# Moving one projection of the cross attention's V from the head of a mixing stage into its gate loop

## The chip, the cores and the metric

The kernel runs on one core of a Trainium2 chip (trn2). The metric is the device time of one execution in microseconds (us). Three executions of the kernel before gave 2055.84, 2061.27 and 2065.23 us, the median is 2061.27 us. The profile is of one further execution, which took 2056.62 us.

## The reference

Two transformer blocks run one after the other on 256 tokens of width 1024, in float32. The second one has two layers, and each layer is this:

```python
x = x + 0.5 * rms_norm(swiglu(rms_norm(x), ffn1_w13[l], ffn1_w2[l]))
h = rms_norm(x, mix_norms[l, 0])
y = token_mixing(h, ...)          # retention, latent attention, differential attention
x = x + rms_norm(y, mix_norms[l, 1])
h = rms_norm(x, cross_norms[l, 0])
m = rms_norm(mem, cross_norms[l, 2])          # 256 memory tokens, not dependent on x
x = x + rms_norm(cross_attention(h, m, cross_wq[l], cross_wkv[l], cross_wo[l]))
x = x + 0.5 * rms_norm(swiglu(rms_norm(x), ffn2_w13[l], ffn2_w2[l]))
```

At the end of token_mixing three branches are gated, added and projected:

```python
proj = einsum('bsnw,nwd->bsnd', branches, w_branch)   # three branches, 512 -> 1024 each
gates = sigmoid(gate_logits)                          # 3 x 1024 columns of h @ w_in
return sum(gates * proj, axis=n) @ w_out
```

In cross_attention `kv = m @ w_kv` has 2048 columns: K of four heads of 256 columns, then V of four heads. It needs the memory alone, so it can be computed long before h is known.

## The kernel before, in words

**Products.** Each float32 operand is split into a high part (`wh`, a cast to fp32r on ACT, L209) and a low part (`wl`, the rest, by DVE, L210). A product is three matmuls: high*high, and the two mixed ones (`mm3`, L242 to L244). In `proj_fm` the weights are the stationary operand and 256 tokens are streamed; in `proj_tm` the tokens are stationary (two halves of 128, t = 0 and t = 1) and up to 512 weight columns are streamed.

**Weights.** `weights` (L213) loads 512 KB into one of three buffers `raw` with a DMA that SP issues, and splits it into one of three buffers `wh` and `wl`. The three are shared by everything outside the inner part of the feed-forward stages. `self.parts` says in how many pieces a tile is split (PK = 4 gives two pieces of 128x512 for a tile of two 512-column rows, PM = 1 gives one of 128x1024).

**K and V ahead of time.** `kv_job` (L1013) holds a list of chunks of `kv`. Chunks 0 to 3 are K of a head each; chunk 4 is V of heads 0 and 1: 512 columns for both halves of tokens, 8 steps of the contraction, 48 matmuls of 128x512 in all, into two banks of PSUM with the tag "p", then two copies on ACT (L1021) to `raw40` and `raw41`. `fill(n)` computes the next n chunks. `run` calls fill(2) in the feed-forward stage before (chunks 0, 1), fill(2) at the head of the layer's first feed-forward (2, 3) and fill(6) at the head of `mix2`, which is chunk 4, since no other is left. Chunk 5 is computed within `cross`.

**mix2.** `norm_T` normalizes and transposes the tokens: squares on ACT and DVE (L335), the root on POOL (L343), the scaling on DVE (L351), 16 transposes on PE (L368), and the split of their result into `xth` and `xtl`. Then comes the fill, then `mla_low` (a `proj_tm` of 416 columns), the projections and the three attentions. At the end stand the gates: for branch 2, four times `gate` and four times `branch`; then, for branches 1 and 0 and each jj of four, `gate` (48 matmuls of 128x256, weights in two tiles, a tanh on ACT) and `branch` (24 matmuls, one tile, two operations on DVE). `ret_att`, which branch 0 needs, is given high priority. `merge` and the product with `w_out` follow.

**What sets the order.** The engines run in order. The order on each engine is set when the kernel is built, by a scheduler that takes instructions by their place in the program where their operands are ready by its own estimate of time; `high_priority` moves a place ahead. Buffers of a tag go round in the program's order.

Of the kernel before, what the change touches and what calls it, by code (L numbers as in the profile page):

```python
# [16 lines left out]
D = 1024  # L17
KD = 8
# [4 lines left out]
P1, PC, PF, PM, PK = 1, 2, 2, 1, 4  # L23
NEARLY = 4
STAG = 120
TAIL = 3
FTAIL = 3
TAILS = (3, 6)
# [82 lines left out]
class Core:  # L111
# [134 lines left out]
    def mm(self, out, a, b, start=True, stop=True):  # L246
        self.nc.tensor.matmul(out, a, b, start=start, stop=stop, skip_group_check=True)  # L247
# [56 lines left out]

    def down_all(self, xt, src, ntail=TAIL):
        with self.pool("tail", ntail) as pool:
            acc, step = self.down_steps(src, len(xt), pool, ntail)
            for k in range(len(xt)):
                step(k, xt[k])
        return acc  # L310
# [180 lines left out]

    def cross(self, xs, gx, w_q, w_o, mt, w_kv, raw, mid=None, ntail=TAIL):

# [477 lines left out]
    def mix1(self, gate_pool, load, early, side):  # L971
# [5 lines left out]
        with self.pool("m1") as pool, self.wides():  # L977
# [19 lines left out]
            for hf in range(2):  # L997
                with self.tc.high_priority(offset=self.tc.cur_priority - start - hf * STAG):
                    self.rwkv(lup[hf], krv[hf], hf, zp[:, 2 * hf:2 * hf + 2, :])
# [13 lines left out]
    def kv_job(self, mt, w_kv, raw):  # L1013

        todo = list(raw)

        def fill(n):
            for _ in range(min(n, len(todo))):
                i = todo.pop(0)
                for r, b in zip(raw[i], self.kv_chunk(mt, w_kv, i)):  # L1020
                    self.nc.scalar.copy(out=r.rearrange("p i c -> p (i c)"), in_=b)  # L1021

        return fill

    def run(self, out):
        a, nc = self.a, self.nc
        n2 = a["cross_norms_2"]
        side = ExitStack()
        mem = {}

        def open_side():
            self.rawp = side.enter_context(self.pool("raw", side="right"))
            self.pad(self.rawp, 224)
            mem["R"] = self.mkR(side.enter_context(self.pool("mt", side="right")))

        def early(pool):
            mem["mt"] = self.norm_T(self.load_x(a["mem"][0]), a["norm_mem_g"][0])
            mem["raw"] = {i: [pool.tile([128, 2, T], F32, name="raw_b1%d" % i)] for i in range(NEARLY)}
            self.kv_job(mem["mt"], a["w_ckv"][0], mem["raw"])(8)

        def prepare(l):

            mt = self.mem_T(a["mem_2"][0], n2[l, 2], mem["R"])
            rt = lambda n: self.rawp.tile([128, 2, T], F32, tag=n, name=n)
            raw = {i: [rt("raw%d%d" % (i, j)) for j in range(1 if i < 4 else 2)] for i in range(5)}
            mem.update(mt=mt, raw=raw, fill=self.kv_job(mt, a["cross_wkv_2"][l], raw))

        fill = lambda n: mem["fill"](n)

        def start_ffn():  # L1050
            fill(2)
            self.rope_tables()

        with self.pool("b1") as pool:
            with self.pool("gt") as gp:
                xs = self.mix1(gp, lambda names: self.load_const(names, pool), lambda: early(pool), open_side)
            with self.pool("cr") as cp:
                self.phase(cp)
                acc = self.cross(xs, a["norm_x_g"][0], a["w_cq"][0], a["w_co"][0], mem["mt"], a["w_ckv"][0],
                                 mem["raw"], mid=lambda: prepare(0))  # L1060
            xs = self.residual(xs, acc)
            acc = self.ffn(xs, a["norm_ffn_g"][0], a["w_ffn_in"][0], a["w_ffn_out"][0], self.conv_hidden,
                           start_ffn)
        xs = self.final_norm(self.residual(xs, acc), a["norm_final_g"])
        with self.pool("b2") as pool:
            self.load_const(["ret"], pool)
            for l in range(2):
                acc = self.ffn(xs, a["ffn1_norms_2"][l, 0], a["ffn1_w13_2"][l], a["ffn1_w2_2"][l], self.swiglu_hidden,
                               lambda: fill(2))
                xs = self.residual(xs, acc, a["ffn1_norms_2"][l, 1], 0.5)  # L1070
                acc = self.mix2(l, xs, lambda: fill(6))
                xs = self.residual(xs, acc, a["mix_norms_2"][l, 1])
                with self.pool("cr") as cp:
                    self.phase(cp)
                    acc = self.cross(xs, n2[l, 0], a["cross_wq_2"][l], a["cross_wo_2"][l], mem["mt"],
                                     a["cross_wkv_2"][l], mem["raw"], mid=(lambda: prepare(1)) if l == 0 else side.close, ntail=TAILS[l])
                xs = self.residual(xs, acc, n2[l, 1])
                acc = self.ffn(xs, a["ffn2_norms_2"][l, 0], a["ffn2_w13_2"][l], a["ffn2_w2_2"][l], self.swiglu_hidden,
                               (lambda: fill(2)) if l == 0 else None)
                xs = self.residual(xs, acc, a["ffn2_norms_2"][l, 1], 0.5)  # L1080
        for t in range(2):
            for h in range(2):
                s = slice(h * 512, (h + 1) * 512)
                nc.sync.dma_start(out=out[t * 128:(t + 1) * 128, s], in_=xs[t][:, s])
# [274 lines left out]
        V.tensor_tensor(out=o, in0=o, in1=sg.rearrange("p t (h c) -> p (t h) c", h=4), op=ALU.mult)  # L1359
        self.to_branch(bp, o, 1)  # L1360

    def mix2(self, l, xs, fill):
        nc, a = self.nc, self.a
        xt = self.norm_T(xs, a["mix_norms_2"][l, 0])
        self.parts = PK
        fill()
        self.parts = PM
        w_in = a["w_in_2"][l]
        with self.pool("m2") as pool, self.wides():
            self.pad(pool, 448)  # L1370
            R = self.phase(pool)
            bps = [Pair(R("bh", [128, 4, T], F32R, 2), R("bl", [128, 4, T], F32R, 2)) for n in range(3)]
            low = self.mla_low(l, xt)
            nlam = self.diff_lam(l)
            dft = R("dft", [128, 8, T])
            for q in range(2):
                bs = self.proj_tm(self.wcols(w_in, 1952 + q * 512, 512), xt, 512)
                self.rotated(bs, dft[:, q * 4:q * 4 + 4, :], 8, 8, 48, 0)
            heads = self.mla_half(l, low, 0)
            self.mla_att(heads, bps[1][:, 0:2, :])  # L1380
            dv = self.tokens(w_in, 2976, xt)
            self.diff_att(l, dft, dv, nlam, bps[2])
            rft = self.s4([128, 4, T], F32, "rft")
            self.rotated(self.proj_tm(self.wcols(w_in, 0, 512), xt, 512), rft, 8, 32, 0, 1)
            heads = self.mla_half(l, low, 1)
            self.mla_att(heads, bps[1][:, 2:4, :])
            rv = self.tokens(w_in, 512, xt)
            sg = self.ret_gate(l, xt)
            order = (2, 1, 0)
            gates = {}  # L1390

            def gate(n, jj):
                b = self.proj_fm(self.wcols(w_in, 3488 + n * D + jj * 256, 256), xt)
                g = R("gm" if n == order[0] else "gate", [128, 2, T], bufs=4 if n == order[0] else 2)
                nc.scalar.activation(out=g.rearrange("p i c -> p (i c)"), in_=b, func=AF.Tanh, scale=0.5)
                gates[n, jj] = g

            def branch(n, jj):
                y = [bps[n][:, k, :] for k in range(4)]
                b = self.proj_fm(self.wcols(a["w_branch_2"][l, n], jj * 256, 256, 4), y)  # L1400
                g, m = gates[n, jj], gates[order[0], jj]
                nc.vector.scalar_tensor_tensor(out=g, in0=g, scalar=1.0, in1=b.rearrange("p (i c) -> p i c", i=2),
                                               op0=ALU.add, op1=ALU.mult)
                if n != order[0]:
                    nc.vector.tensor_tensor(out=m, in0=m, in1=g, op=ALU.add)

            start = self.tc.cur_priority
            for jj in range(4):
                gate(order[0], jj)
            for jj in range(4):  # L1410
                branch(order[0], jj)
            with self.tc.high_priority(offset=self.tc.cur_priority - start):
                self.ret_att(rft, rv, sg, bps[0])
            for n in order[1:]:
                for jj in range(4):
                    gate(n, jj)
                    branch(n, jj)
            merged = self.merge([gates[order[0], jj] for jj in range(4)])
        return self.down_all(merged, a["w_out_2"][l])

# [41 lines left out]
```

## Time and profile before

| | |
|---|---|
| the profiled execution | 2056.62 us, of it 2054.8 us from the first to the last instruction |
| median of three executions | 2061.27 us |
| TensorE (PE) busy | 1994.9 us, 97% |
| weight load (PEld) busy | 1831.4 us, 89% |
| VectorE (DVE) busy | 1320.3 us, 64% |
| ScalarE (ACT) busy | 1093.4 us, 53% |
| GpSimd (POOL) busy | 45.4 us, 2% |
| DMA queue of the loads | 350.60 MB, 55.3% of 16 engines' span |
| mean granted clock of TensorE | 0.993 |

PE is busy for almost the whole span, and the chain that ended last is 86% PE. Busy time of PE counts each matmul from its start to its modelled end, and these overlap, so the times at which matmuls start tell more than their durations: a steady stream of 128x512 matmuls starts one every 0.23 us, though each is shown as 0.39 us long.

### The profile page before, as it was taken

What the parts mean: (1) busy time and instruction counts of PE and PEld (TensorE: products, weight loads), DVE (VectorE), ACT (ScalarE), POOL (GpSimd) and SP (SyncE); (2) the same over time, 40 slices, a digit from 0 to 9 for tenths busy, and PEclk for the clock granted to TensorE, in tenths of its full rate; (3) what the DMA queues carried; (4) which work ended last, traced back from release to release, by engine and by line L of the source; (5) the groups of instructions that cost most, each with busy time, mean ns of one, the idle gap of its engine ahead of it and who ended that gap; (6) DMA issues with size and microseconds to landing.
All of it is one profiled execution on the core that took longest, in us unless ns stands there. A gap on an engine that the chain in (4) does not pass through costs nothing.

```text
span 2054.8 us, 36137 instructions
## 1 busy us (share of the span) xinstructions
PE 1994.9 (97%) x14508; PEld 1831.4 (89%) x14508; DVE 1320.3 (64%) x2183; ACT 1093.4 (53%) x2014; POOL 45.4 (2%) x65
## 2 busy tenths in 40 slices
PE   7999999999999999999999999999999999998998
PEld 6989978899999998789988999999987899888997
DVE  6896566766675566666677655655576656765555
ACT  5763345655564456654456544544466544554444
POOL 0000000000000001000000000000000000000000
PEclk9999999999999999999999999999999999999999
DMA  6432255666666654436665666656635456645663
GB/s 200 145 120 85 90 188 181 224 189 187 186 217 190 193 174 144 138 113 175 200 203 182 218 194 196 204 184 190 196 117 154 122 159 187 204 154 174 194 193 106
DMA packets 259033, 352.92 MB, mean 172 GB/s; under 512 B 12336, under 2 KB 214448, under 8 KB 258864
## 3 DMA queue, kind: packets, MB, share of 16 engines
q1 hardware_dynamic: 258864, 350.60, 55.3%
q8 instruction: 114, 1.87, 0.4%
q14 instruction: 55, 0.45, 0.1%
HBM read 349.50 MB, written 1.05 MB: 171 GB/s over the span
## 4 chain that ended last, share of the span: by engine, by line
PE 86%; DVE 6%; ACT 3%; DMA 3%; issue 1%; POOL 0%; SPq 0%; DVEq 0%; POOLq 0%; ACTq 0%
PE bp L242 20%; PE bp L243 20%; PE bp L244 19%; PE acc L242 6%; PE acc L243 6%; PE acc L244 6%; PE a L247 3%; DVE wl L210 2%; ACT wh L209 1%; PE bc L247 1%; DMA raw<-in_w_in_dram 1%; PE bc L368 1%; DMA raw<-in_cross_wkv_dram 1%; PE bc L1137 1%; DMA raw<-in_cross_wo_dram 1%
## 5 line engine op out<-in xcount | busy, mean ns | idle before, releaser
L210 DVE TENSOR_TENSOR wl<-raw,wh 128x512 fp32r<-128x512 f32 (+2 forms) x1082 | 797.0, 774 | 523.0 <-ACT wh L209 512.4
L209 ACT CAST wh<-raw 128x512 fp32r<-128x512 f32 (+2 forms) x1082 | 699.7, 688 | 701.4 <-PE bp L243 486.6
L242 PE MATMUL bp<-xth,wh 128*128 128x256 f32 x2704 | 759.7, 281 | 8.1 <-ACT xth L209 4.8
L244 PE MATMUL bp<-xth,wl 128*128 128x256 f32 x2704 | 756.5, 280 | 5.5 <-DVE wl L210 5.4
L243 PE MATMUL bp<-xtl,wh 128*128 128x256 f32 x2704 | 756.8, 280 | 2.7 <-DVE xtl L210 2.7
L242 PEld LDWEIGHTS bp<-xth,wh 128*128 128x128 f32 x2704 | 512.4, 190 | 19.6 <-ACT xth L209 6.4
L244 PEld LDWEIGHTS bp<-xth,wl 128*128 128x128 f32 x2704 | 511.7, 189 | 11.3 <-DVE wl L210 6.9
L243 PEld LDWEIGHTS bp<-xtl,wh 128*128 128x128 f32 x2704 | 511.2, 189 | 6.8 <-DVE xtl L210 4.0
L243 PE MATMUL acc<-wl,hh 128*128 128x512 f32 x440 | 172.9, 393 | 0.0
L244 PE MATMUL acc<-wh,hl 128*128 128x512 f32 x440 | 170.9, 391 | 0.0
L242 PE MATMUL acc<-wh,hh 128*128 128x512 f32 x440 | 142.7, 393 | 0.0
L242 PE MATMUL bp<-wh,xth 128*128 128x512 f32 (+1 forms) x256 | 98.7, 400 | 2.3 <-DVE tmd L1132 1.4
L243 PE MATMUL bp<-wl,xth 128*128 128x512 f32 (+1 forms) x256 | 100.5, 396 | 0.0
L244 PE MATMUL bp<-wh,xtl 128*128 128x512 f32 (+1 forms) x256 | 99.2, 393 | 0.0
L244 PEld LDWEIGHTS acc<-wh,hl 128*128 128x128 f32 x440 | 82.7, 188 | 15.0
L243 PEld LDWEIGHTS acc<-wl,hh 128*128 128x128 f32 x440 | 82.8, 188 | 14.3
L242 PEld LDWEIGHTS acc<-wh,hh 128*128 128x128 f32 x440 | 79.2, 188 | 14.1
L343 POOL TENSOR_TENSOR rr<-rv,mhalf 128x1 f32<-128x1 f32 x46 | 30.1, 656 | 1644.8 <-DVE rv L341 1644.3
L242 PEld LDWEIGHTS bp<-wh,xth 128*128 128x128 f32 x256 | 47.3, 188 | 13.3 <-ACT tmd L1282 2.2
L243 PEld LDWEIGHTS bp<-wl,xth 128*128 128x128 f32 x256 | 48.2, 188 | 9.2 <-DVE wl L210 0.8
L244 PEld LDWEIGHTS bp<-wh,xtl 128*128 128x128 f32 x256 | 48.2, 188 | 8.4
L244 PE MATMUL bp<-bh,wl 128*128 128x256 f32 x192 | 54.0, 281 | 0.0
(377 smaller groups left out, 2578.7 us busy)
## 6 DMA issues: line engine op xcount, KB each, us to landing
raw<-in_ffn_w_dram SPq DMA_DIRECT2D x264, 512.0 KB, 4.4
raw<-in_w_in_dram SPq DMA_DIRECT2D x134, 512.0 KB, 3.7
raw<-in_w_ffn_in_dram SPq DMA_DIRECT2D x44, 512.0 KB, 4.6
raw<-in_cross_wkv_dram SPq DMA_DIRECT2D x32, 512.0 KB, 4.4
raw<-in_w_branch_dram SPq DMA_DIRECT2D x24, 512.0 KB, 3.8
raw<-in_w_ffn_out_dram SPq DMA_DIRECT2D x22, 512.0 KB, 4.2
raw<-in_w_ckv_dram SPq DMA_DIRECT2D x16, 512.0 KB, 4.7
raw<-in_w_out_dram SPq DMA_DIRECT2D x16, 512.0 KB, 4.2
```

What stands on the lines that cost most here:

```text
L209: first = self.nc.scalar.copy(out=h, in_=src)
L210: self.nc.vector.tensor_tensor(out=l, in0=src, in1=h.bitcast(F32), op=ALU.subtract)
L242: mm(out, a.h, b.h, start=start, stop=False, skip_group_check=True)
L243: mm(out, a.h, b.l, start=False, stop=False, skip_group_check=True)
L244: mm(out, a.l, b.h, start=False, stop=stop, skip_group_check=True)
L247: self.nc.tensor.matmul(out, a, b, start=start, stop=stop, skip_group_check=True)
L343: nc.gpsimd.tensor_tensor(out=r, in0=v, in1=self.mhalf[:, :1], op=ALU.pow)
L368: nc.tensor.transpose(b[:, j * 128:(j + 1) * 128], xn[:, k * 128:(k + 1) * 128], self.ident)
L1137: self.nc.tensor.transpose(b[0:s.shape[1], i * 128:(i + 1) * 128], s, self.ident)
```

## The change

fill at the head of `mix2` is asked for 0 chunks in both layers, so chunk 4 is left in the list. A new generator `few` computes it: the same 48 matmuls, but with both halves of tokens taken for each weight tile of two steps, into two banks with the tag "c", and with a pause after each four matmuls. In the loop over branches 1 and 0 one step of it is taken behind each `gate` and one behind each `branch`: 16 places, of which the first 12 take four matmuls each, the 13th the two copies. Each of its four weight tiles is asked for by the first of its three steps, and split in one piece, since `parts` is PM there.

```diff
+FILL = (0, 0)
...
+        def few():
+            i = todo.pop(0)
+            bs = [self.bank("c") for _ in range(2)]
+            v = w_kv.rearrange("(k p) n -> p k n", p=128)
+            c0 = D + (i - 4) * 512
+            mm = self.nc.tensor.matmul
+            n = 0
+            for k0 in range(0, KD, 2):
+                w = self.weights(v[:, k0:k0 + 2, c0:c0 + 512], 2, 512)
+                for t in range(2):
+                    for k in (k0, k0 + 1):
+                        x, y = mt[k][:, t * 128:(t + 1) * 128], w[:, k - k0, :]
+                        for q, (l, r) in enumerate(((x.h, y.h), (x.h, y.l), (x.l, y.h))):
+                            mm(bs[t], l, r, start=k == 0 and q == 0, stop=k == KD - 1 and q == 2, skip_group_check=True)
+                            n += 1
+                            if n % 4 == 0:
+                                yield
+            for r, b in zip(raw[i], bs):
+                self.nc.scalar.copy(out=r.rearrange("p i c -> p (i c)"), in_=b)
+            yield
+        return fill, few
...
-                acc = self.mix2(l, xs, lambda: fill(6))
+                acc = self.mix2(l, xs, lambda: fill(FILL[l]), mem["jobs"][1])
...
+            more = few()
             with self.tc.high_priority(offset=self.tc.cur_priority - start):
                 self.ret_att(rft, rv, sg, bps[0])
             for n in order[1:]:
                 for jj in range(4):
                     gate(n, jj)
+                    next(more, None)
                     branch(n, jj)
+                    next(more, None)
+            for _ in more:
+                pass
```

## Rows read from the trace of the kernel before

**Rows 1.** The page: shares of the chain that ended last, by engine.

```profile
PE 86%; DVE 6%; ACT 3%; DMA 3%; issue 1%; POOL 0%; SPq 0%; DVEq 0%; POOLq 0%; ACTq 0%
```

**Rows 2.** Stretches, layer 0: window, length, busy (x count) by engine, clock, DMA share, GB/s.

```profile
788.00:800.00 12.00, 11.79 (x59) 9.48 (x58) 11.26 (x23) 10.14 (x23) 2.49 (x3) 1.00 0.34 102
...
980.00:1012.00 32.00, 32.00 (x274) 32.00 (x273) 19.65 (x21) 15.02 (x17) 0.00 (x0) 1.00 0.67 195
```

**Rows 3.** Timeline of PE, head of mix2, layer 0: start, length, line, operands, shape.

```profile
781.23 0.39 PE L242 MATMUL bp<-wh,mth 128*128 128x512 f32 x1
...
788.10 0.39 PE L242 MATMUL bp<-wh,mth 128*128 128x512 f32 x1
...
794.74 0.40 PE L244 MATMUL bp<-wh,mtl 128*128 128x512 f32 x1
794.97 0.60 PE L368 MATMUL bc<-c_ident,xn 128*128 128x128 f32 x4
...
799.01 0.46 PE L242 MATMUL bp<-wh,xth 128*128 128x416 f32 x1 [0.21 <-ACT raw L1021]
```

**Rows 4.** Timeline of PE, the same place in layer 1.

```profile
1519.13 0.39 PE L242 MATMUL bp<-wh,mth 128*128 128x512 f32 x1
...
1530.05 0.46 PE L242 MATMUL bp<-wh,xth 128*128 128x416 f32 x1 [0.21 <-ACT raw L1021]
```

**Rows 5.** Timelines of ACT and DVE, head of mix2, layer 0.

```profile
785.09 0.60 ACT L335 ACTIVATE x<-acc 128x512 f32<-128x512 f32 x1 [5.21 <-PE acc L244]
...
791.74 1.41 DVE L351 SCALAR_TENSOR_TENSOR xn<-x,rr,g 128x512 f32<-128x512 f32 x2
...
800.37 0.58 ACT L209 CAST xth<-bc 128x512 fp32r<-128x512 f32 x1
...
801.44 0.68 DVE L210 TENSOR_TENSOR xtl<-bc,xth 128x512 fp32r<-128x512 f32 x1
```

**Rows 6.** Timeline of PE before the last feed-forward stage, which has no fill.

```profile
1854.77 0.39 PE L244 MATMUL acc<-wh,kvl 128*128 128x512 f32 x1
1859.96 1.94 PE L368 MATMUL bc<-c_ident,xn 128*128 128x128 f32 x8 [4.80 <-DVE xn L351]
1863.35 1.97 PE L368 MATMUL bc<-c_ident,xn 128*128 128x128 f32 x8 [1.45 <-DVE xtl L210]
1865.14 0.79 PE L242 MATMUL bp<-xth,wh 128*128 128x256 f32 x2
```

**Rows 7.** Stretches, PE alone: window, length, busy (x count), granted clock, DMA share, GB/s.

```profile
1858.00:1859.00 1.00, 0.00 (x0) 0.50 0.98 309
1867.00:1868.00 1.00, 1.00 (x7) 0.54 0.08 16
...
1057.00:1061.50 4.50, 2.06 (x12) 1.00 0.92 291
1062.50:1065.50 3.00, 3.00 (x16) 0.50 1.02 404
...
1792.50:1793.00 0.50, 0.50 (x7) 1.00 0.92 303
...
269.00:269.50 0.50, 0.50 (x2) 0.50 0.00 0
273.50:274.00 0.50, 0.50 (x4) 0.61 0.00 0
```

**Rows 8.** Timelines of PE, ACT and DVE: one gate and one branch, layer 0.

```profile
954.64 0.28 PE L242 MATMUL bp<-xth,wh 128*128 128x256 f32 x1
...
960.30 0.28 PE L242 MATMUL bp<-bh,wh 128*128 128x256 f32 x1
...
963.12 0.28 PE L242 MATMUL bp<-xth,wh 128*128 128x256 f32 x1
...
958.97 1.05 ACT L209 CAST wh<-raw 128x1024 fp32r<-128x1024 f32 x1 [2.28 <-PE bp L243]
...
964.73 1.22 DVE L210 TENSOR_TENSOR wl<-raw,wh 128x1024 fp32r<-128x1024 f32 x1
```

More of the change, by code (lines that the diff above doesn't have):

```diff
@@ L1021, in fill @@
                     self.nc.scalar.copy(out=r.rearrange("p i c -> p (i c)"), in_=b)
-        return fill
+        def few():
[19 more added lines that the diff above has]
+        return fill, few
     def run(self, out):
@@ L1038, in early @@
             mem["raw"] = {i: [pool.tile([128, 2, T], F32, name="raw_b1%d" % i)] for i in range(NEARLY)}
-            self.kv_job(mem["mt"], a["w_ckv"][0], mem["raw"])(8)
+            self.kv_job(mem["mt"], a["w_ckv"][0], mem["raw"])[0](8)
         def prepare(l):
@@ L1045, in prepare @@
             raw = {i: [rt("raw%d%d" % (i, j)) for j in range(1 if i < 4 else 2)] for i in range(5)}
-            mem.update(mt=mt, raw=raw, fill=self.kv_job(mt, a["cross_wkv_2"][l], raw))
-        fill = lambda n: mem["fill"](n)
+            mem.update(mt=mt, raw=raw, jobs=self.kv_job(mt, a["cross_wkv_2"][l], raw))
+        fill = lambda n: mem["jobs"][0](n)
         def start_ffn():
@@ L1360, in ret_att, with mix2 @@
         self.to_branch(bp, o, 1)
-    def mix2(self, l, xs, fill):
+    def mix2(self, l, xs, fill, few):
         nc, a = self.nc, self.a
```

## The prediction

> **What bounds the kernel now.** I read the chain that ended last first: 86% of it is PE [rows 1]. Then I read the two places that the change touches, as stretches. The head of `mix2` (788 to 800 us) has PE busy for 11.79 of 12 us, and the gate loop (980 to 1012) for 32.00 of 32 us, at the full granted clock [rows 2]. Busy time hides small gaps, so I next read where matmuls start. In the gate loop one gate and one branch, 72 matmuls, take 963.12 - 954.64 = 8.48 us [rows 8], 0.118 us each without a hole; the pattern repeats with that period. So the stage that receives the 48 matmuls has no free time on PE. The stage that gives them up is different in kind: behind the last matmul of the feed-forward accumulation nothing of `mix2` can start on PE until the normalization has gone through ACT, DVE and POOL, and what stands in PE's queue in that time is chunk 4, from 788.10 until the first product of the new tokens at 799.01 [rows 3]. Layer 1 shows the same, 1519.13 to 1530.05 [rows 4]. The work that is moved away is the cover of this wait.
>
> **The change part by part, for one layer.**
>
> *The moved work.* Thirty matmuls of chunk 4 start between 788.10 and 794.74 [rows 3], 6.64 / 29 = 0.229 us apart. The 48 cost 48 x 0.229 = 11.0 us of PE, the same in the new place since shape and count are the same. Added in the gate loop, where PE is full: +11.0 us. Taken from the head: as much as is not replaced by waiting.
>
> *What the head becomes.* Six of the 48 already stand within the feed-forward tail, from 781.23 [rows 3]; without them the accumulation, and with it the whole chain behind it, ends 6 x 0.229 = 1.4 us earlier. PE then ends its last accumulating matmul at 788.1 - 1.4 = 786.7. The chain itself isn't shortened: the squares of the first half of tokens start at 785.09, as soon as that half is accumulated, and the scaling of these tokens by DVE runs from 791.74 in two pieces of 0.7 us [rows 5]. Today's transposes come at 794.97 only because they queue behind chunk 4; their operand is there at 791.74 + 0.7 = 792.4, which is 791.0 after the shift. So PE stands idle from 786.7 to 791.0, 4.3 us. Four transposes take 0.60 us, a cast to `xth` 0.58, and the low part `xtl`, which the third matmul needs, 0.68 [rows 3, 5]: 0.60 + 0.58 + about 0.1 of handing over brings the first product to 792.3, and 0.68 holds the third until 793.0. Of these 2.0 us some 0.8 are transposes and first products. Idle: 4.3 + 1.2 = 5.5 us. Lower bound 4.3, the first stretch alone. Upper bound from the one comparable head without a fill: from 1854.77 + 0.23 to 1865.14, 10.1 us with 16 transposes in it that a waiting product needs all of [rows 6]; less 16 transposes at 0.60 us for four [rows 3] 7.7 us. I stay near the lower one, since `proj_tm` can begin with one half of tokens and so needs eight transposes only. PE has 24 matmuls of 128x416 of the first half before it needs the second. Weights are no limit there: three buffers that now hold chunk 4's tiles would hold `w_in` early. Today's own small wait at 799.01 (0.21 idle, 0.4 by starts, behind a copy to `raw` [rows 3]) goes away: -0.4 us.
>
> *The clock.* Behind the idle stretch of rows 6 the granted clock is 0.50, the 1.2 GHz level, at 1858 and still so until about 1867.9 [rows 7]; the products from 1865.14 on ran at half rate for 2.8 us and lost 1.4. In the cross attention of layer 0 PE was busy for 2.06 of 4.5 us (1057.0 to 1061.5), and then from 1062.5 to 1065.5 the clock was at half with PE busy: 1.5 us lost. The largest loss is in the first block: half rate with PE busy from 269.0 to about 273.9, 2.4 us lost. On the other side, the same place as the second case kept 1.00 in layer 1, at 1792.5 [rows 7]. The bounds are 0 and 2.4 us; the new idle stretch, 4.3 us in one piece, is nearest to that of rows 6 (4.80 us before the transposes), behind which the clock fell, so I take the mean of the three that fell, 1.7 us.
>
> The Trainium skill (TensorE: Matmul & The Clock Gate, section "Why this matters for your kernels") advises against idle gaps between bursts of matmuls, because the clock falls to half behind them. That rule speaks against this change; by it both layers pay the 1.7 us, by the row that kept 1.00 neither would, a difference of 3.4 us in all.
>
> *Weight buffers in the loop.* A tile of `few` holds one of three buffers for three steps, so gate (two tiles) and branch (one) share two. Now: a gate starting at 954.64 frees its first tile at its 36th matmul, 958.9, the next split starts at 958.97, and its low part is done about 1.05 + 1.23 us later plus handing over, 2.4 us behind the release (the cast length is in rows 8, the subtraction has the same length as the row at 964.73). With two buffers the branch's tile is split in that place: released at 4.24 us behind the gate's start, ready at 6.6; needed at 5.66 + 0.92 (four of few) + 0.24 = 6.8. The next gate's second tile waits for the branch to end at 9.4 and for DVE, which first has the branch's two operations (today the subtraction starts 1.6 us behind the branch's end, 964.73 against 963.12 [rows 8]): ready at 9.4 + 1.6 + 1.2 = 12.2, needed at 10.3 + 12 x 0.118 + 0.24 = 12.0. So each step is just met or missed by some 0.2 to 0.3 us, and the next four products of `few` may stand in. Price: 0 at best; at worst, if in all six rounds in which `few` holds a buffer PE waits for DVE's two operations before a subtraction, 6 x 1.6 = 9.6 us. I take 1.5 us. DMA sees the same bytes, some 3.7 tiles in 10.3 us for 3 in 8.5, about the same rate. ACT and DVE lose eight half-size splits at the head and get four whole ones in the loop; both have slack in either stretch [rows 2]. The copies behind the 13th step are needed only in the cross attention.
>
> *The sum.* Head: -11.0 + 5.5 + 1.7 - 0.4 = -4.2 us. Loop: +11.0 + 1.5 = +12.5 us. Net +8.3 us in a layer, +16.6 us in both. Against the profiled execution that is 2056.6 + 16.6 = 2073.2 us, its span 2071.4; this execution is 4.7 us below the median of the runs. Against the median: 2061.3 + 16.6, about **2077 us**. About 0.5%, 10 us, is what a measurement of this kernel can tell from no change.
>
> **The rivals.**
>
> *The clock holds and the gap is the short one.* PE waits 4.3 us, the clock keeps 1.00 as in layer 1's cross attention [rows 7], and the loop meets every buffer. Per layer 4.3 - 0.4 = 3.9, in all +8 us: 2069 us, not slower by what can be told. It decides in the form that the short gap doesn't bring the clock down; against it stands that of the four places in rows 7 three fell, the one with the gap nearest to this among them.
>
> *The products are hidden.* They need the memory, a weight tile and two banks only, so the scheduler may put them where PE would wait in the attentions or in `ret_att`, and then the loop doesn't grow by 11.0. For it: they are asked for in small pieces. Against it: PE has no holes in the loop [rows 2, 8], and their weight tiles queue behind those of all the projections before. If all 11.0 were hidden: -4.2 us per layer, 2053 us, still within 0.5%; half of them give +2.6 us.
>
> *The buffers become the bound.* Each round waits as at worst above: +9.6 in place of 1.5 us, net 16.4 per layer, 2094 us. It would show as PE waiting for `wl` or `wh` in the loop; it decides where the subtraction of the second gate tile ends later than PE gets to its 12th matmul plus what `few` can put in.
>
> **How the numbers follow.** My forecast (+10 to +24 us) has 0.60, the clock that holds 0.18, the hidden products 0.09, the buffers as bound 0.13. The range takes in the short gap in full or in part and the buffers for the most part: 2064 to 2092 us. Slower by over 0.5%: 0.60 + 0.13 = 0.73; within: 0.18 and most of the hidden case, 0.23; faster: 0.04.
>
> **What would show it.** Right: between the last accumulating matmul and the first transposes PE idle for over 4 us, waiting for DVE `xn` (L351), in both layers; granted clock at 0.50 somewhere in the following 8 us; the distance from the first gate of branch 1 to the start of `w_out` longer by 11 to 13 us; the start of the `xth` products about 4 us earlier against the feed-forward before. Wrong: chunk 4's matmuls early in the attentions; a gate loop that grows by clearly less than 11.0 us; a head where another chunk of work stands in the gap; a loop with waits for `wl` of over 5 us in sum.

## The result, and the profile after

The changed kernel takes 2071.45 us (median of 7 runs, 2066.84 to 2075.21), the kernel before 2057.36 in the same rounds: ratio 1.0059 [1.0045, 1.0073]. Later rounds gave 2074.60 against 2058.20, ratio 1.0078 [1.0064, 1.0092]. So it is slower, by 12 us in the one set and 16 us in the other (by the ratios; 14 and 16 by the medians). The profiled execution of the changed kernel took 2066.84 us with a span of 2064.8. Its line numbers are one higher than before up to line 1020 (L243 is L242 of before).

The page of the changed kernel, share of the chain that ended last by engine, answers [rows 1]. Nothing in it tells of the change:

```profile
PE 86%; DVE 6%; ACT 3%; DMA 2%; issue 1%; POOL 0%; DVEq 0%; SPq 0%; POOLq 0%; ACTq 0%
```

To see where time goes I use four instructions of each layer that both kernels have, as marks on PE's timeline: A is the last 128x256 product ahead of the last accumulations of the feed-forward, B the first 128x512 product of `mix2` (the head lies between A and B), C the first product of `w_out` (the attentions and the gate loop lie between B and C), and D the first transposes of the next norm. PE's timeline of the kernel before, layer 0 (start, length, line, operands, shape):

```profile
776.08 0.28 PE L244 MATMUL bp<-xth,wl 128*128 128x256 f32 x1
...
809.09 0.40 PE L242 MATMUL bp<-wh,xth 128*128 128x512 f32 x1
...
1022.49 1.10 PE L242 MATMUL acc<-wh,mh 128*128 128x512 f32 x4
...
1053.29 1.04 PE L368 MATMUL bc<-c_ident,xn 128*128 128x128 f32 x8
```

The same four in the changed kernel:

```profile
773.36 0.28 PE L245 MATMUL bp<-xth,wl 128*128 128x256 f32 x1
...
803.77 0.40 PE L243 MATMUL bp<-wh,xth 128*128 128x512 f32 x1
...
1026.02 0.62 PE L243 MATMUL acc<-wh,mh 128*128 128x512 f32 x2
...
1056.24 1.03 PE L369 MATMUL bc<-c_ident,xn 128*128 128x128 f32 x8
```

A to B is 33.01 us before and 30.41 after, B to C 213.40 and 222.25, C to D 30.80 and 30.22. The same marks, in all kernels of this study, which are told one by one below (difference to before in us, layer 0 / layer 1):

| kernel | A to B, head | B to C, with the loop | C to D | A to D |
|---|---|---|---|---|
| before, first trace | 33.01 / 33.00 long | 213.40 / 213.39 long | 30.80 / 30.80 long | |
| before, second trace (f0) | 0.00 / +0.01 | -0.01 / -0.01 | 0.00 / 0.00 | -0.01 / 0.00 |
| changed, first trace | -2.60 / -2.54 | +8.85 / +8.89 | -0.58 / -0.58 | +5.67 / +5.77 |
| changed, second trace (g2) | -1.56 / -2.48 | +8.82 / +8.95 | -0.58 / -0.58 | +6.68 / +5.89 |
| e1, products taken out | -1.41 / -1.77 | +0.47 / +1.03 | -0.55 / -0.55 | -1.49 / -1.29 |
| e2, products in both places | 0.00 / +0.01 | +8.81 / +8.81 | -0.58 / -0.58 | +8.23 / +8.24 |
| e3, idle products, first form | -3.29 / -3.26 | +8.62 / +8.69 | -0.56 / -0.58 | +4.77 / +4.85 |
| e4, half of the products moved | -3.82 / -3.79 | +4.40 / +4.40 | -0.55 / -0.55 | +0.03 / +0.06 |
| g1, idle products in the gap | -3.88 / -3.87 | +8.52 / +8.56 | -0.58 / -0.58 | +4.06 / +4.11 |
| f1, two idle products in the loop | -0.04 / +0.01 | -2.29 / -2.26 | -0.58 / -0.58 | -2.91 / -2.83 |
| f2, twelve in the loop | -0.04 / +0.01 | +2.54 / +2.52 | -0.55 / -0.56 | +1.95 / +1.97 |
| f3, one in the loop | -0.04 / 0.00 | +0.23 / +0.25 | -0.56 / -0.56 | -0.37 / -0.31 |

The reader is to see two things. These stretches repeat to 0.01 us between the two traces of before, so tenths mean something here. And the rest of the kernel does not repeat like this: outside of the stretches A to D the two traces of before differ by 3.7 us in all. The second is 2.15 us longer between the first and the second norm of the first block and 2.32 us longer in the attention over the memory of layer 0, and a little shorter elsewhere; granted clocks of 0.66 and 0.83 stand in different places in the two.

**The head.** PE's timeline of the changed kernel, layer 0, answers [rows 3]:

```profile
783.78 0.39 PE L245 MATMUL acc<-wh,hl 128*128 128x512 f32 x1
788.93 1.78 PE L369 MATMUL bc<-c_ident,xn 128*128 128x128 f32 x8 [4.76 <-DVE xn L352]
790.52 0.71 PE L243 MATMUL bp<-wh,xth 128*128 128x416 f32 x1
791.04 0.55 PE L244 MATMUL bp<-wl,xth 128*128 128x416 f32 x1
792.61 1.11 PE L369 MATMUL bc<-c_ident,xn 128*128 128x128 f32 x4 [1.02 <-DVE xtl L211]
793.37 0.69 PE L245 MATMUL bp<-wh,xtl 128*128 128x416 f32 x1
```

and layer 1, which answers [rows 4]:

```profile
1520.96 0.39 PE L245 MATMUL acc<-wh,hl 128*128 128x512 f32 x1
1526.10 1.78 PE L369 MATMUL bc<-c_ident,xn 128*128 128x128 f32 x8 [4.76 <-DVE xn L352]
1527.61 0.71 PE L243 MATMUL bp<-wh,xth 128*128 128x416 f32 x1
```

Where chunk 4 stood, PE waits 4.76 us for `xn`, and then again 1.02 us, now for `xtl`. The transposes take 1.78 us for eight where before's four took 0.60. Stretches of the changed kernel (window, length, busy (x count) of PE, PEld, DVE, ACT and POOL, granted clock, DMA share, GB/s) tell why:

```profile
785.00:795.00 10.00, 5.05 (x19) 4.07 (x20) 8.37 (x19) 5.67 (x13) 2.18 (x3) 0.71 0.11 32
790.00:800.00 10.00, 8.98 (x41) 8.00 (x39) 4.19 (x9) 4.13 (x7) 0.50 (x1) 0.70 0.00 0
...
1520.00:1530.00 10.00, 4.12 (x17) 2.62 (x16) 9.33 (x21) 6.81 (x18) 2.20 (x4) 0.82 0.12 40
1530.00:1540.00 10.00, 10.00 (x49) 9.80 (x49) 3.93 (x6) 4.13 (x5) 0.00 (x0) 0.84 0.04 6
```

The head of before is at 1.00 [rows 2]; here the granted clock is 0.70 in the mean of ten us, and 0.82 and 0.84 in layer 1. The two layers differ by the place of the windows alone: at 1530 us they cut the fall of layer 1 in two. In either layer the clock stands at 0.50, the 1.2 GHz level, for 6.8 us (stretches, PE alone: window, length, busy, granted clock, DMA share, GB/s):

```profile
789.17:796.00 6.83, 5.81 (x22) 0.50 0.00 0
...
1526.45:1533.28 6.83, 5.71 (x21) 0.50 0.01 2
```

**The loop.** PE's timeline of the changed kernel, first added piece, layer 0; [rows 8] answer it:

```profile
954.85 0.28 PE L245 MATMUL bp<-xth,wl 128*128 128x256 f32 x1
954.97 0.40 PE L1038 MATMUL bc<-wh,mth 128*128 128x512 f32 x1
955.20 0.40 PE L1038 MATMUL bc<-wl,mth 128*128 128x512 f32 x1
...
957.54 0.39 PE L1038 MATMUL bc<-wh,mtl 128*128 128x512 f32 x1
957.77 0.28 PE L243 MATMUL bp<-bh,wh 128*128 128x256 f32 x1
```

The products don't come four at a time: the scheduler put them into the stream in four pieces of twelve, two of them parted ten and two by two products of the loop (957.77 - 954.97 = 2.80 us for the first). No instruction of PE in this loop waits. The groups of PE in the same 32 us of [rows 2] (line, engine, operands, shape, count, busy us, mean ns of one, idle before), the kernel before first:

```profile
L242 PE MATMUL bp<-xth,wh 128*128 128x256 f32 x64 | 18.0, 281 | 0.0
```

and the changed kernel:

```profile
L243 PE MATMUL bp<-xth,wh 128*128 128x256 f32 x54 | 14.9, 276 | 0.0
L1038 PE MATMUL bc<-wl,mth 128*128 128x512 f32 x8 | 3.1, 394 | 0.0
```

One product of the same shape takes 276 ns in place of 281, and it starts 113.3 ns behind the one before it in place of 117.8 (by starts: 24 of before take 2.83 us, 24 of after 2.72). The reader is to look at this mean: the 4.5 ns between the two paces, on some 500 products, are why the loop grew by 8.9 us though 11.1 were put in (the first piece 2.80 us, the other three 2.75 each).

### The profile page after: what moved, and what is told of

The parts are those of the page before. It is cut to its first block, busy times and chain, and to the rows that moved or that the text cites. A ratio compares the mean times of both kernels' runs of the same rounds, so it can differ in the third digit from the quotient of the medians.

```text
span 2064.8 us, 36109 instructions
## 1 busy us (share of the span) xinstructions
PE 1994.0 (97%) x14508; PEld 1830.4 (89%) x14508; DVE 1320.4 (64%) x2175; ACT 1094.9 (53%) x2006; POOL 44.9 (2%) x65
## 4 chain that ended last, share of the span: by engine, by line
PE 86%; DVE 6%; ACT 3%; DMA 2%; issue 1%; POOL 0%; DVEq 0%; SPq 0%; POOLq 0%; ACTq 0%
PE bp L243 19%; PE bp L244 19%; PE bp L245 19%; PE acc L243 6%; PE acc L244 6%; PE acc L245 6%; PE a L248 3%; DVE wl L211 2%; PE bc L248 1%; ACT wh L210 1%; PE bc L1038 1%; DMA raw<-in_w_in_dram 1%; DVE xn L352 1%; PE bc L369 1%; PE bc L1160 1%
## 5 line engine op out<-in xcount | busy, mean ns | idle before, releaser
L211 DVE TENSOR_TENSOR wl<-raw,wh 128x512 fp32r<-128x512 f32 (+3 forms) x1074 | 796.0, 778 | 533.8 <-ACT wh L210 522.1
L210 ACT CAST wh<-raw 128x512 fp32r<-128x512 f32 (+3 forms) x1074 | 700.4, 694 | 707.3 <-PE bp L244 481.2
L243 PE MATMUL bp<-xth,wh 128*128 128x256 f32 x2704 | 759.2, 281 | 7.9 <-ACT xth L210 4.4
L243 PEld LDWEIGHTS bp<-xth,wh 128*128 128x128 f32 x2704 | 511.8, 189 | 19.7 <-ACT xth L210 6.0
L243 PE MATMUL acc<-wh,hh 128*128 128x512 f32 x440 | 142.7, 393 | 0.0
L243 PE MATMUL bp<-wh,xth 128*128 128x512 f32 (+1 forms) x256 | 100.1, 404 | 1.9 <-DVE tmd L1155 1.4
L243 PEld LDWEIGHTS acc<-wh,hh 128*128 128x128 f32 x440 | 79.1, 188 | 14.1
L369 PE MATMUL bc<-c_ident,xn 128*128 128x128 f32 x224 | 37.6, 310 | 29.4 <-DVE xn L352 23.7
L369 PEld LDWEIGHTS bc<-c_ident,xn 128*128 128x128 f32 x224 | 29.3, 158 | 36.2 <-DVE xn L352 18.6
L243 PEld LDWEIGHTS bp<-wh,xth 128*128 128x128 f32 x256 | 48.5, 192 | 12.4 <-ACT tmd L1305 2.2
```

Source lines behind the costliest of these rows:

```text
L210: first = self.nc.scalar.copy(out=h, in_=src)
L211: self.nc.vector.tensor_tensor(out=l, in0=src, in1=h.bitcast(F32), op=ALU.subtract)
L243: mm(out, a.h, b.h, start=start, stop=False, skip_group_check=True)
L369: nc.tensor.transpose(b[:, j * 128:(j + 1) * 128], xn[:, k * 128:(k + 1) * 128], self.ident)
```

## The experiments

**The head alone (e1).** The products are taken out of the loop, four small ones stand in for them.

```diff
-            for k0 in range(0, KD, 2):
-                w = self.weights(v[:, k0:k0 + 2, c0:c0 + 512], 2, 512)
-                for t in range(2):
-                    for k in (k0, k0 + 1):
...
+            for t in range(2):
+                for h in range(2):
+                    mm(bs[t][:, h * T:(h + 1) * T], mt[0].h[:, t * 128:(t + 1) * 128], mt[h].h, ...)
```

> The changed kernel with chunk 4's 48 products left out of the gate loop (four products of 128x256 and the two copies stand in, V of heads 0 and 1 is not computed). What is left is the head without its fill. Theory: the head gives back only what the wait and the fallen clock leave of 11.0 us, 3.5 us in layer 0 and 2.1 in layer 1 by the two traces, less 0.5 us a layer for the four products: 4 to 5 us below the kernel before, and a clock of 0.50 behind both heads. Rival, all of the moved work was on the path and the gap is covered by something else: 22 us below. Rival, the gap costs as much as the fill: same as before.

Measured: 2058.47 us against 2057.05, ratio 1.0005 [0.9995, 1.0015]: no change that can be told. By the marks the head gains 1.41 and 1.77 us only, for work of 11.0 us that is gone. In layer 1 another 0.6 of that goes behind B, in a wait for `tmd` of 1.24 us where the kernel before waits 0.68; the clock is back at 1.00 by then:

```profile
1553.55 0.47 PE L243 MATMUL bp<-wh,xth 128*128 128x512 f32 x1 [1.24 <-DVE tmd L1150]
```

The granted clock (stretches of e1, layer 0) stayed down longer than in the changed kernel, into the second of these windows:

```profile
790.00:800.00 10.00, 5.53 (x20) 4.67 (x21) 8.24 (x19) 5.39 (x13) 2.18 (x3) 0.65 0.09 30
800.00:810.00 10.00, 10.00 (x48) 9.68 (x47) 4.11 (x6) 4.57 (x8) 0.00 (x0) 0.84 0.16 39
```

So chunk 4 at the head of the kernel before costs next to nothing: without it PE waits, and then pays for having waited. The theory's -4 to -5 us are not there: the marks give -2.8 in the two layers, the times +1.0.

**The loop alone (e2).** The head of before is kept, and the loop computes chunk 4 a second time.

```diff
-FILL = (0, 0)
+FILL = (1, 1)
...
-            i = todo.pop(0)
+            i = 4
```

> The kernel before with chunk 4 computed at the head as it was, and computed a second time in the gate loop by the new generator. What is added is the loop's part of the change alone. Theory: 11.0 us of products a layer, less the 2.1 to 2.2 us by which gates and branches run faster behind a burst of 128x512: 17 to 18 us above the kernel before, no fall of the clock at the heads. Rival, each product costs its 11.0 us in full plus waits for buffers: 22 to 25 us above. Rival, the products find free time: under 5 us above.

Measured: 2079.59 us, ratio 1.0104 [1.0091, 1.0117], 21.4 us. The marks give +8.81 for the loop and -0.58 behind it, 16.5 us in the two layers, a little under the theory's 17 to 18; not a trace of hiding. By the time alone the rival with 22 to 25 us isn't excluded (the interval is 19 to 24 us), but its waits for buffers are not there: PE waits no longer between B and C than before (0.82 us in all). The other 5 us stand outside: against the first trace of before 2.65 at the start, 2.64 in the attention over the memory of the first block (granted clock 0.83 in 370 to 380 us), 1.80 in that of layer 0. Such differences also stand between two traces of before, so I don't put them down to the edit, but that wasn't shown for this kernel.

**Idle products, first form (e3).**

```diff
+        b = self.bank("p")
+        for q in range(18):
+            nc.tensor.matmul(b, self.mw[:, q % 2, 0:128], self.mw[:, 0:2, :].rearrange("p a c -> p (a c)"), ...)
         self.parts = PM
```

> The changed kernel with 18 products of 128x512 on finished tokens of the memory, whose result nobody reads, at the place where the fill stood; about 12 of them fall into the gap, 2.7 us. They do no work, they only keep PE from standing idle in one piece. Theory: the granted clock stays at 1.00 behind both heads, which saves 1.5 to 2 us a layer, less 1.4 us a layer for the six products that the order puts into the feed-forward tail: 0 to 2 us below the changed kernel, and the granted clock at 1.00 through both heads. Rival, the clock falls regardless: 2 to 3 us above the changed kernel.

Measured: 2069.86 us, ratio 1.0051 [1.0036, 1.0065], inside the expected 0 to 2 below the changed kernel, and too near to it to be told apart. Six of the 18 went into the feed-forward's tail, where they put off the last accumulation by 1.4 us (6 x 0.229); the rest covered half of the gap:

```profile
790.00:800.00 10.00, 8.41 (x37) 6.66 (x36) 7.09 (x17) 5.11 (x12) 2.17 (x3) 0.83 0.12 33
```

The clock fell for a shorter time (the mean of these ten us is 0.83), and the head became 0.7 us shorter than that of the changed kernel, though its last accumulation came later. Not all of that is the clock: the order on DVE is another one here, and the second wait of the head is gone (shown below, where the prediction is gone through). So a form was needed without the six (g1); it has the order of the changed kernel.

**Half of the products (e4).** V of head 0 stays at the head, V of head 1 goes into the loop, in 128x256 products.

```diff
+        def first():
+            i = todo.pop(0)
+            bs = self.proj_tm(self.wcols(w_kv, D, 256), mt, 256)
...
-                w = self.weights(v[:, k0:k0 + 2, c0:c0 + 512], 2, 512)
+                w = self.weights(v[:, k0:k0 + 4, D + 256:D + 512], 4, 256)
```

> V of head 0 (256 columns, 48 products of 128x256, 5.5 us) stays at the head, V of head 1 goes into the gate loop in the same way, four products a step. Theory: 5.5 us cover the gap of some 5 us, so PE idles under 1 us and the clock holds; the head is 5 us shorter than before, the loop 5.5 us longer less up to 2.2 us if gates and branches run faster there as well: between 4 us below the kernel before and the same time. Rival, the wait comes back in part since the transposes queue behind the products: 3 to 6 us above.

Measured: 2059.43 us, ratio 1.0011 [1.0001, 1.0022], 2.3 us slower than before, at the edge between the two expectations. By the marks it is a draw (+0.03 and +0.06): the head gains 3.8 us for 5.5 us of work taken away, with the clock at 1.00 in all stretches from 780 to 810 us, and the loop loses 4.4. The first half of chunk 4 is what covers the wait; only the second half could be moved at all, and there is no room for it in the loop.

**A second trace of before (f0).** No edit.

> This is the kernel before once more, for a second trace of it. Three of the four kernels run so far show a start (first to second norm) that is 1.4 to 2.6 us longer than in the first trace of the kernel before, although nothing is changed there. Theory: that is the clock's fall at 100 to 120 us and the transfers of that run, no work of the kernels; then this trace too shows about +2 us there, and granted clocks near 0.66 instead of 0.83 in the stretch from 110 us, and its 128x256 products in the gate loop again run at 117.8 ns from the first to the last. Rival: the start really is longer in the changed kernels; then this trace agrees with the first to 0.3 us.

Measured: one execution of 2060.24 us. The start is 2.15 us longer than in the first trace and the clock in the stretch from 110 us is 0.66, as the theory expects; a longer start comes up in a kernel without any edit, so it needs no edit. The loop is at 281 ns per product again:

```profile
L242 PE MATMUL bp<-xth,wh 128*128 128x256 f32 x63 | 17.7, 281 | 0.0
```

**What makes the loop's pace (f1, f2, f3).** The kernel before with two, twelve and one products of 128x512 in the first gate of the second branch; nobody reads what they write.

```diff
                 for jj in range(4):
                     gate(n, jj)
+                    if n == order[1] and jj == 0:
+                        self.burst(self.lastw.h, 2)
                     branch(n, jj)
...
+    def burst(self, w, n):
+        b = self.bank("c")
+        for q in range(n):
+            self.nc.tensor.matmul(b, w[:, q % 2, 0:128], w[:, 0:2, :].rearrange("p a c -> p (a c)"), ...)
```

> The kernel before, with two products of 128x512 that nobody reads put into the gate loop of each layer, in its first gate of the second branch; nothing else is changed and nothing is left out. It asks why the loop of the changed kernel grew by 8.9 us where its added products alone took 4 x 2.75 = 11.0. Theory: the 128x256 products have two paces (117.8 ns in the whole loop of before, 113.3 ns in the loop of after from the first added piece on), and wide products are what switches the pace; then the loop behind the two products runs at 113.3 ns, which is worth some 65 us x 3.8% = 2.5 us per layer, less 2 x 0.23 for the two products: about -2 us per layer, -4 us in all (2053). Rival: the pace belongs to what the added V products bring with them (their weights' transfers, the splits, the order of the gates); then it stays at 117.8 ns and the time rises by 2 x 0.47 = 0.9 us (2058).

> As the run with two products, with twelve of 128x512 at once, as many as one piece of the added V products (12 x 0.229 = 2.75 us per layer). Theory (wide products switch the pace): the loop behind them at 113.3 ns, so +2.75 - 2.5 per layer, about +0.5 us in all. Rival (the pace belongs to what comes with the V products): 117.8 ns throughout, +2.8 per layer, +5.6 us in all. If twelve switch it and two don't, the length of the piece is what counts.

> As the run with two products, with a single one of 128x512. Theory (wide products switch the pace): one is enough, 113.3 ns behind it, -2.2 us per layer. Rival A (it stays at 117.8 ns): +0.23 us per layer. Rival B (an odd number against an even one decides): this run and the one with two differ in the pace behind the burst.

Measured, two products: 2054.58 us against 2057.94, ratio 0.9979 [0.9970, 0.9989]. More work and less time, and the theory's -4 us almost to the number (by the marks -4.5 in the two loops, and -1.2 in the two stretches behind them, which the theory didn't have); this is the one kernel here that beats both. Twelve products: one execution of 2069.60 us; one product: 2057.36. The groups of PE from 980 to 1012 us with two products:

```profile
L243 PE MATMUL bp<-xth,wh 128*128 128x256 f32 x63 | 17.4, 276 | 0.0
```

with twelve, which the scheduler placed as three and nine:

```profile
L243 PE MATMUL bp<-xth,wh 128*128 128x256 f32 x59 | 16.6, 281 | 0.0
```

and with one:

```profile
L243 PE MATMUL bp<-xth,wh 128*128 128x256 f32 x61 | 17.1, 281 | 0.0
```

So what the V products bring with them (transfers, splits) isn't needed for the other pace, and two wide products do it without. But "wide products switch the pace" falls as a rule: behind one, three and nine of them the 128x256 products of the loop went on at 117.8 ns. They did something all the same. In the stretch C to D, 132 products of 128x512 that no edit touches, every kernel with anything put into the loop is 0.55 to 0.58 us faster than the two traces of before: 228.9 ns per product in place of 233.3, also where the loop before it kept the slow pace (f2, f3, e1 and the end of e4). So a pace need not pass from one shape to the next. Rival B, that odd and even decide, agrees with these four pieces as far as the loop goes. It does not fit the changed kernel, whose first piece of twelve changed the pace and whose later pieces, all even, did not change it back, nor e1, where four products of 128x256 left it as it was, while in e4 the first 24 of that shape changed it and the second 24 changed it back. What decides is open.

**Idle products in the gap alone (g1), and the changed kernel beside it (g2).** The idle products read the last hidden tile, so that they can't start before the feed-forward's end.

```diff
+            if cover:
+                b, w = self.bank("p"), pend[-1].h
+                for q in range(20):
+                    self.nc.tensor.matmul(b, w[:, q % 2, 0:128], w.rearrange("p a c -> p (a c)"), ...)
         self.raws = self.wp
         return acc
```

> The changed kernel, with 20 products of 128x512 that nobody reads put at the head of each layer's mixer: they read the last hidden tile of the feed-forward stage, so the built order has 18 of them (18 x 0.229 = 4.1 us) in the wait between the last accumulation and the first transposes, which is 5.15 us long in the changed kernel, and 2 in the wait of 0.7 us just before. Nothing is left out. It takes the clock's fall away and leaves the waits. In the changed kernel the clock fell to 0.70 in the ten us behind the head, and its first products, 2.45 us ahead of those of before when they start, are 0.7 to 0.9 us behind after 12 us: by that count the fall cost 3.2 to 3.4 us per layer, twice the 1.7 that the prediction took. Theory: with the wait filled the clock stays at 1.00 and the 3.2 us per layer come back: 6 us less than the changed kernel in all, about 1.0028 of before. Rival A (the prediction's size was right, and the rest is idle time of another kind): 1.7 per layer, about 1.0042. Rival B (the products get in the way of the transposes, or the clock falls all the same): no better than the changed kernel, 1.0055 to 1.007.

> The changed kernel once more, on the same chip as the run beside it, so that the two can be compared in the same rounds: theory and rivals alike expect its first ratio again, 1.0059 within 0.0015, with the clock at 0.65 to 0.85 in the ten us behind each head, 8.2 to 8.3 us more from the first transposes of the mixer to the next cross attention's norm than before, less 0.0 to 0.3 us for chance, and the same pace of 113.3 ns in the gate loop behind the first added piece.

Measured: 2071.31 us (1.0065 [1.0051, 1.0079]) with the cover, 2074.60 (1.0078 [1.0064, 1.0092]) without, in the same rounds: 3.3 us by the medians, 2.7 by the ratios, for 40 products more. The two intervals overlap, and 1.0065 taken by itself lies in rival B's range, since both kernels of this set lie higher; so the times alone don't decide, and the traces have to. The ratio of the changed kernel is above the 1.0059 it had, by more than the 0.0015 that I allowed; its loop came out as expected, its second trace has a longer head in layer 0 and, against the first trace of before, 3.5 us more in the attention over the memory of layer 1. PE's timeline of g1:

```profile
785.91 0.39 PE L245 MATMUL acc<-wh,hl 128*128 128x512 f32 x1
786.14 4.25 PE L435 MATMUL bp<-hh 128*128 128x512 f32 x18
791.06 1.32 PE L369 MATMUL bc<-c_ident,xn 128*128 128x128 f32 x8 [0.67 <-DVE xn L352]
792.39 0.46 PE L243 MATMUL bp<-wh,xth 128*128 128x416 f32 x1
792.69 0.35 PE L244 MATMUL bp<-wl,xth 128*128 128x416 f32 x1
794.54 0.66 PE L369 MATMUL bc<-c_ident,xn 128*128 128x128 f32 x4 [1.50 <-DVE xtl L211]
794.95 0.44 PE L245 MATMUL bp<-wh,xtl 128*128 128x416 f32 x1
```

and its stretches:

```profile
785.00:795.00 10.00, 7.81 (x39) 5.73 (x37) 8.57 (x17) 5.39 (x16) 2.72 (x4) 1.00 0.12 33
795.00:805.00 10.00, 10.00 (x56) 9.77 (x55) 6.63 (x16) 7.08 (x11) 0.07 (x1) 1.00 0.20 55
```

The transposes wait exactly as long behind the last accumulation as in the changed kernel (5.15 us by starts in both), but with PE busy for most of it the clock stays at 1.00 and the products behind run at full rate. The head is 29.13 us long in both layers, of which the two idle products ahead of the last accumulations cost 0.48. Without these it is 28.65, and the four heads of the changed kernel (30.41, 30.46, 31.45, 30.52) are longer by 1.8, 1.8, 2.8 and 1.9 us. That is the price of the fall, by the trace of one kernel with the cover. The head with 2.8 us is the one in which the clock stayed low for 10.2 us; in the other three it was 6.8. My 3.2 falls: I had read it from how far the first products came behind those of before, and part of that way is the wait for `xtl`, 1.50 us, that stays when the clock is up. Rival A's 1.7 is what came back.

## Why the prediction was right, and where it was off

The prediction has the direction and the mechanism, and with +16.6 us a size near the 12 and 16 us measured. That it came so near is in part luck. Its sum per layer, +8.3 us, was too large against 5.7, 5.8, 6.7 and 5.9 in the traces; the loop was put 4.2 us too high and the head's gain 1.7 us too high, and the two errors partly cancel. The two layers' marks add up to 11.4 and 12.6 us only, and the rest of what the times show stands outside of the places that the prediction is about. (The sum 2061.3 + 16.6 gives 2078, not 2077, and the mean of the three clock losses is 1.8, not 1.7; neither matters.) Term by term:

| term, us per layer | predicted | measured |
|---|---|---|
| products in the loop | +11.0 | +11.1, nothing hidden |
| buffer waits in the loop | +1.5 | 0.0 |
| pace of the products behind the first piece | not in the sum | -2.2 to C, -0.6 from C to D |
| loop | +12.5 | +8.3 |
| products out of the head | -11.0 | -11.0 |
| waiting in their place, with the small wait that goes away | +5.1 | +6.6 (33.01 - 28.65 = 4.4 us gained) |
| clock | +1.7 | +1.8, +1.8, +2.8, +1.9 |
| head | -4.2 | -2.6, -2.5, -1.6, -2.5 |

- *What bounds the kernel.* Right. PE has no free time in the loop, and the 48 products cost there what they cost anywhere. The products are not hidden, so the rival with 2053 us is out.
- *The first wait in the head.* The accumulation ends 1.4 us earlier, as worked out: A to the last accumulation is 783.78 - 773.36 = 10.42 us after and was 11.79 before. The idle time from there was put at 4.3 us and is 4.76. The step that failed slightly is that the whole chain of the norm moves by 1.4 us: DVE's scaling [rows 5] moved by 0.9 against A. Why not by 1.4 was not followed.
- *The second wait.* This step failed. It let four transposes and then 0.68 us of `xtl` stand between `xn` and the third product, which would start 2.0 us behind the transposes' operand. The scheduler put eight transposes first and four of the second half ahead of the third product, and `xtl` doesn't follow its cast. DVE's timeline of the changed kernel:

```profile
788.12 1.41 DVE L352 SCALAR_TENSOR_TENSOR xn<-x,rr,g 128x512 f32<-128x512 f32 x2
...
790.54 1.42 DVE L352 SCALAR_TENSOR_TENSOR xn<-x,rr,g 128x512 f32<-128x512 f32 x2 [0.48 <-POOL rr L344]
791.87 0.68 DVE L211 TENSOR_TENSOR xtl<-bc,xth 128x512 fp32r<-128x512 f32 x1
```

  The first `xtl` stands in DVE's queue behind the scaling of the second half of the tokens, which itself waits for POOL. So the half that was ready could not be used. In g1, at full clock, the third product starts at 794.95, 3.9 us behind the transposes. With the first wait this makes 6.6 in place of 5.1 us. That it is the order shows in e3, where DVE makes this `xtl` before the second half's `xn`, and PE has no transposes ahead of the third product:

```profile
794.93 0.69 DVE L211 TENSOR_TENSOR xtl<-bc,xth 128x512 fp32r<-128x512 f32 x1 [0.18 <-ACT xth L210]
795.54 1.40 DVE L352 SCALAR_TENSOR_TENSOR xn<-x,rr,g 128x512 f32<-128x512 f32 x2
...
795.68 0.71 PE L245 MATMUL bp<-wh,xtl 128*128 128x416 f32 x1
```

  Its transposes start at 793.62, so the third product is 2.06 us behind them, the 2.0 us that the prediction had, and no wait over 0.1 us stands between. The prediction counted each operation's length and left out what stands ahead of it in an engine's queue; it also spoke of slack on DVE, which [rows 2] have busy for 11.26 of 12 us at the head of before.
- *The clock.* Right in kind in both layers, and 1.7 us was a good size: 1.8 where the trace of the changed kernel was first taken. In all four heads it went to 0.50 behind the 4.76 us of idle time, and g1, which fills most of the gap with work that nobody needs and stays at 1.00, shows that the gap does it. The Trainium skill (TensorE: Matmul & The Clock Gate, section "Why this matters for your kernels") has the rule against idle gaps between bursts of matmuls that the prediction names; the traces agree with it in these four heads. The rival with the clock that holds is out here. The row that spoke for it, the place in layer 1's cross attention that kept 1.00 [rows 7], did not hold in the second trace of the same kernel (f0; PE alone):

```profile
1796.40:1797.40 1.00, 1.00 (x7) 0.50 0.74 197
```

  One trace was too little to put a chance on it.
- *The buffers.* The 1.5 us were an estimate between 0 and 9.6 and the measurement is 0: no instruction of PE in the loop waits for `wl` or `wh`. The rounds were worked out for four products at a time, and they came in pieces of twelve. With twelve at once DVE and ACT have some 2.75 us to get ahead, which may be the reason; it wasn't tried. The rival with 2094 us is out.
- *What was missing.* The pace. The whole loop of before ran at 117.8 ns per product, and I took this rate [rows 8] as what such a product costs. The loop of the changed kernel runs at 113.3, and so does that of before with two idle products in it. I named a loop that grows by clearly less than 11.0 us as what would make the prediction wrong, and it did grow by less, 8.9; but not because products were hidden.

What stays open: what decides which of the two paces a stretch has; and the 1 to 5 us by which most timed differences lie above the sums of the two layers' marks (e2: 21.4 against 16.5; g1: 13.4 against 8.2; e4: 2.3 against 0.1). They stand where the traces of one kernel differ among themselves. A part is in the attention over the memory: from D to the first transposes of the next norm the two layers take 140.6 and 142.6 us together in the two traces of before, 147.6 in g1, and 146.9 in f2, which leaves chunk 4 where it was. So it doesn't need the moved work; what makes it was not found.

## What to carry to other kernels

Before moving work out of a place where it "only" fills a wait, take it out without putting it anywhere: here 11 us of products per layer taken away gained 1.5 us at most by the marks and nothing by the times, so no new place on an engine without holes could win anything. A wait that opened on PE here cost its length, what queues ahead of each link of the chain that ends it, and the clock behind it. And a duration that repeats through a whole stretch need not be what the instruction costs; look for the same shape elsewhere in the trace and see if it is always the same.

## What the runs showed of the hardware that I had not expected

Products of one shape have two steady paces at the same granted clock of 1.00: 128x256 start every 113.3 or every 117.8 ns, 128x512 every 228.9 or every 233.3 ns (the products of `w_out`, after and before). A stretch keeps its pace over hundreds of products and over changes of tiles; where the pace changed, it was at an added piece or where the shape changes. The stretches B to C and C to D of before repeat to 0.01 us in a second trace; so it goes with the program and not with chance. Two products without any use, placed at one point of each layer's loop, brought the other pace to some 60 us behind them and made the kernel faster by 0.2%.

The clock fell at all the heads with the open gap, to the same 0.50, but not for the same time. After the same 4.8 us of idle time it stood there for 6.8 us in both layers of the changed kernel's first trace, for 10.2 us in layer 0 of its second trace and in both layers of e1 (stretches, PE alone, layer 0 of the second trace and of e1):

```profile
790.87:801.11 10.24, 8.42 (x29) 0.50 0.01 5
...
792.95:803.19 10.24, 8.72 (x31) 0.50 0.00 0
```

So one trace of a head gives the price of that fall, 1.8 or 2.8 us, and not of the next.
